# Spreading LayerNorm means and reciprocal roots over the partitions: one fp32 product each, or two float32r products

## The chip, the cores and the metric

One core of a Trainium2 chip runs the whole program in one launch. The metric is the device time of one execution in microseconds (us). The kernel before was run three times: 1618.89, 1621.05 and 1621.62 us, median 1621.05. One more execution was profiled; the trace in this document comes from it.

## What is computed

Two layers of a transformer block act on 256 latent and 256 context tokens with 1024 features, all in fp32. Each layer has a half feed-forward (FFN), a mixer (attention in layer 0, an mLSTM in layer 1) and a second half FFN. After each of these stands a LayerNorm:

```
def post_norm(h, delta, g, b):
    return layer_norm(DEEPNORM_ALPHA * h + delta, g, b)

def layer_norm(x, g, b):
    mu = mean(x); var = mean((x - mu)**2)
    return (x - mu) * rsqrt(var + LN_EPS) * g + b
```

The next stage multiplies the normalised rows, shifted and scaled by a modulation, with its weights. This document is about the means `mu` and the roots `rsqrt(var + eps)`.

## The kernel before, in words

**Layout.** The residual stream lies transposed in SBUF: tile `h` holds 8 blocks (`d`) of 128 features on the partitions by 512 tokens, of which columns 0 to 255 are the latent tokens (LAT) and 256 to 511 the context tokens (CTX). A norm therefore has to sum over partitions, and TensorE (PE) does this by a product with a 128x128 tile whose entries are all equal.

**Products.** A weight or an activation is split into a rounded part and a remainder, both of type float32r (`split`, L228 on ScalarE and L233 on VectorE), and `mm3` makes one accurate product of three float32r products (L244). A plain fp32 product appears in the trace as two MATMUL records and two weight loads. The products of the norms go through the lambda on L458, which also pins them to the order of the program on PE.

**Norms.** `norm` (from L453) is a generator; the other code advances it step by step. There are nine norms, one LAT and one CTX after each of the first four stages and a last one for LAT alone (`alone`). The letters in the step tables are its advances:

- `b` starts a LAT norm, `B` a CTX norm; the next letter `m` makes the product for the mean: `s1` holds the sum of the blocks (for LAT of the first seven, so that the norm can begin before the last block is there), and a 128x128 tile of 1/(1024-128) or 1/1024 sums it over the partitions and spreads the result to all 128 (L473).
- `c`, eight times, takes the mean from one block on VectorE (DVE, L478), squares it on ScalarE (ACT, L485) and adds up squares on DVE or GpSimd (POOL, L495).
- `v` makes the variance with products of one column (L503 to L507); a LAT norm also makes `dl`, the correction for the block left out (L510). Then the reciprocal root is worked out in eight small DVE instructions (L264 to L271), the roots are put on a diagonal `dg` (L521), and for LAT `dl` is copied out of PSUM (L527).
- `r` multiplies a tile of ones with `dg` (L535), which spreads the roots to all partitions.
- `x`, eight times, subtracts `dl` where DVE does it (L546) and makes the operands of the next stage: L551 on DVE, L552 on ACT, L553 on DVE.

**Order.** A planner orders the instructions of each engine by the order in the source and by when their inputs should be ready; pinned instructions keep the order of the source. Where the norm's steps fall among the products is written out by hand in tables. `TAILSTEP` (after the FFN stages) and `MTAILSTEP` (after attention) have keys (0 for LAT or 1 for CTX, block of outputs, index of the product triple); `LEADSTEP`, `ATTSTEP` and `MLSTEP` place the CTX norm among the first products of the next stage, with keys (unit, k). In this way a norm runs on DVE and ACT while PE goes on with the products of the stage that ends or begins.

**Addresses.** `SH`, `SHM` and `SHR` shift the weights in their tiles. Some FFN units go through `fast_in`, seven half products with operands that `fast_operands` lays into three tiles called `made`; behind these a tile of `FLIP` = 56 columns stands unused.

Of the kernel before, what the change touches and what calls it, by code (L numbers as in the profile page):

```python
# [18 lines left out]
P = 128  # L19
D = 1024  # L20
# [10 lines left out]
LINE = 16  # L31
# [57 lines left out]

FAST = {0: (99, 99), 1: (9, 5), 2: (9, 5)}  # L90
RESET = (14, 17, 20)
FLIP = 56
PIECES = 4
DOTS = {
    0: {**{("in", j): 3 for j in range(4, 21)}, **{("out", 0, d): 2 for d in range(8)}, **{("out", 1, d): 1 for d in range(4)}},
# [1 line left out]
    2: {**{("in", j): 3 if j < 3 else 2 for j in range(4)}, **{("out", 0, d): 3 for d in range(6)}, **{("out", 1, d): 2 for d in range(4)}},  # L97
}

TAILSTEP = {(0, 3, 1): 'bmccccccc', (1, 0, 2): 'c', (1, 0, 6): 'v', (1, 1, 9): 'rxxxxxxxx'}  # L100
MTAILSTEP = {(0, 7, 0): 'bmccccccc', (1, 0, 3): 'c', (1, 1, 0): 'v', (1, 6, 0): 'r', (1, 7, 0): 'xxxxxxxx'}

LASTROW = 9
LASTK = 6
# [1 line left out]


LEADSTEP = {
    1: {(0, 0): 'mcccccccc', (2, 1): 'v', (2, 5): 'rxxxxxxxx'},
    2: {(0, 5): 'mcccccccc', (2, 0): 'v', (2, 5): 'rxxxxxxxx'},  # L110
}
ATTSTEP = {(1, 1): 'mcccccccc', (3, 6): 'v', (5, 0): 'rxxxxxxxx'}
MLSTEP = {(1, 0): 'mcccccccc', (3, 4): 'v', (3, 7): 'rxxxxxxxx'}
MIXAT = 20
MLLEAD = 7
FILL = (-1, -1, 1, 7)
# [58 lines left out]
class Body:  # L175
# [99 lines left out]
    def setup(self):  # L275
        nc, a = self.nc, self.a
        self.cols = col = self.t([P, 3 * BLOCK // 2])
        for i, x in enumerate((1.0, 1.0 / D, 1.0 / (D - P), 0.5 / D)):
            nc.vector.memset(col[:, i : i + 1], x)
        self.mean1, self.half = col[:, 1:2], col[:, 3:4]  # L280
        self.ones, self.mean, self.most = (col[:, i : i + 1].broadcast_to([P, P]) for i in range(3))

        self.h = self.t([P, ND, T])
        self.xh = self.t([P, ND, T + BLOCK], F32R)
        self.xl = self.t([P, ND, T + BLOCK], F32R)
        self.ident = self.t([P, P])
        self.vec = self.t([P, V_N])
        self.mod = {}
        self.s1 = {}
        self.waiting = []  # L290
# [146 lines left out]
    def pin(self, ins):  # L437

        return self.tc.keep_in_program_order(ins)
# [14 lines left out]
    def norm(self, g, coef, keep=True, nxt=True, alone=False):  # L454


        nc, V, S = self.nc, self.nc.vector, self.nc.scalar
        mm = lambda *k, **kw: self.pin(nc.tensor.matmul(*k, **kw))  # L458
        t0, t1 = g
        w = t1 - t0  # L460
        n = w // P
        raw = alone and nxt
        v = 0 if t0 == 0 else 1
        most = g == LAT
        cols = lambda x, i: x[:, i * P : (i + 1) * P]
        if raw:
            ce = self.t([P, 2, ND], tag="modv", bufs=12)
            for i in range(2):
                V.tensor_copy(ce[:, i, :], coef()[1 + i][:, v, :])
            ce = ce.rearrange("p i d -> p d i")  # L470
            self.split(ce, self.xh[:, :, T : T + 2], self.xl[:, :, T : T + 2])
        m = self.ps()
        mm(m[:, :w], self.most if most else self.mean, self.s1[g], start=True, stop=True)  # L473
        sums = {}
        for d in range(ND):
            yield
# [2 lines left out]
            if raw:  # L479
                c = coef()[1][:, v, d : d + 1]  # L480
# [18 lines left out]
        last = self.h[:, ND - 1, t0:t1]  # L499
# [6 lines left out]
        x = self.small(n)  # L506
        pin = self.pin  # L507
        if most:
            dl = self.ps()
            mm(dl[:, :w], self.mean, last, start=True, stop=True)  # L510
            c2 = self.small(n)
            for i in range(n):
                c = var[:, n + i : n + i + 1]
                V.tensor_scalar(c2[:, i : i + 1], c, c, -0.5, ALU.mult, ALU.mult)
# [5 lines left out]
        dg = self.tmp(w)  # L520
        pin(V.tensor_tensor(  # L521
            out=dg.rearrange("p (n f) -> p n f", n=n), in0=self.ident[:, None, :].broadcast_to([P, n, P]),
            in1=r[:, :, None].broadcast_to([P, n, P]), op=ALU.mult,
        ))
        if most:
            dls = self.t([P, TL], tag="dl", bufs=1)
            pin(V.tensor_copy(dls, dl[:, :w]))  # L527
# [14 lines left out]
        for d in range(ND):  # L542
# [4 lines left out]
            ab, c, e = coef()  # L547
            x = self.tmp(w)
# [158 lines left out]
    def ffn(self, layer, s, gate, groups, side, start=None):  # L707
# [4 lines left out]
        with self.tc.tile_pool(name=f"ffn{li}", bufs=1) as gp:  # L712
# [35 lines left out]
            for hf in range(2):  # L748
# [1067 lines left out]
```

## Time and profile before

| | |
|---|---|
| median of three runs | 1621.05 us (1618.89 to 1621.62) |
| the profiled execution | 1623.23 us |
| its span, first to last instruction | 1621.5 us |
| PE busy | 1604.2 us, 99% |
| DVE busy | 1377.2 us, 85% |
| ACT busy | 759.1 us, 47% |
| POOL busy | 62.3 us, 4% |
| granted TensorE clock | 0.999 |

In the rows of the profile a line number is that of the kernel above. PE is TensorE multiplying, PEld its weight load, DVE VectorE, ACT ScalarE, POOL GpSimd. A group's row gives what it does, its shapes, how often, its busy time, the mean of one, and the idle time in front of it with what ended it. A busy PE is not PE at its peak, since matmuls overlap: how fast they follow each other is read from starts and counts.

### The profile page before, as it was taken

To read this page: it belongs to the slowest core of one execution; us is meant where nothing else is said; L and a number is where in the kernel's file an instruction comes from. 1 tells how busy PE (TensorE), PEld (TensorE's weight loads), DVE (VectorE), ACT (ScalarE), POOL (GpSimd) and SP (SyncE) were. 2 spreads that over 40 slices of the span, in tenths; PEclk is the share of its full clock that TensorE was granted. 3 is DMA by queue.
4 is the path that set the end of the run, shared out by engine and by line. 5 is a ranking of instruction groups with operands and counts; after the bars stand their busy time and mean duration, and the time that the engine had idled before them with its cause. 6 is when DMAs were issued, how large, how long until landed. Compare 5 with 4: busy or idle time off the path is not lost. (4 is left out here: it accounts for less than half of the span.)

```text
span 1621.5 us, 26945 instructions
## 1 busy us (share of the span) xinstructions
PE 1604.2 (99%) x10424; PEld 1453.2 (90%) x10424; DVE 1377.2 (85%) x2783; ACT 759.1 (47%) x1344; POOL 62.3 (4%) x77
## 2 busy tenths in 40 slices
PE   9999999999999999999999999999999999999998
PEld 7888888889988998989999998889989889999986
DVE  7789989878879879689986979689978958897687
ACT  6522132224676344515662435326643657566542
POOL 0000000001011200000000100000001000020000
PEclk9999999999999999999999999999999999999999
DMA  9667777642203342542254262743362332537552
GB/s 359 219 211 226 255 232 244 207 143 86 66 1 94 115 143 66 195 156 105 105 190 148 79 189 72 251 178 106 130 233 86 117 105 92 158 99 252 178 174 91
DMA packets 71648, 249.49 MB, mean 154 GB/s; under 512 B 7896, under 2 KB 10712, under 8 KB 71520
## 3 DMA queue, kind: packets, MB, share of 16 engines
q1 hardware_dynamic: 70944, 246.99, 46.6%
q8 instruction: 81, 1.33, 0.3%
q10 hardware_dynamic: 576, 0.79, 0.1%
q14 instruction: 47, 0.39, 0.1%
HBM read 246.69 MB, written 1.05 MB: 153 GB/s over the span
## 5 line engine op out<-in xcount | busy, mean ns | idle before, releaser
L244 PE MATMUL t<-t,t 128*128 128x256 f32 (+2 forms) x8484 | 1303.8, 315 | 4.9 <-ACT t L552 1.3
L244 PEld LDWEIGHTS t<-t,t 128*128 128x128 f32 x8484 | 1178.1, 188 | 116.4 <-DVE t L553 2.1
L228 ACT CAST t<-t 128x512 fp32r<-128x512 f32 (+3 forms) x573 | 436.4, 785 | 480.2 <-PE t L244 153.1
L233 DVE TENSOR_TENSOR t<-t,t 128x256 fp32r<-128x256 f32 (+3 forms) x792 | 516.7, 690 | 107.9 <-ACT t L228 106.0
L361 DVE SCALAR_TENSOR_TENSOR t<-t,t 128x1024 bf16<-128x1024 f32 x224 | 260.6, 1220 | 0.2
L974 PE MATMUL t<-t,t 128*128 128x256 f32 (+1 forms) x256 | 79.4, 310 | 0.1
L976 PE MATMUL t<-t,t 128*128 128x256 f32 (+1 forms) x256 | 78.6, 307 | 0.1
L975 PE MATMUL t<-t,t 128*128 128x256 f32 (+1 forms) x256 | 78.2, 306 | 0.0
L599 ACT ACTIVATE t<-t 128x256 f32<-128x256 f32 (+1 forms) x67 | 32.1, 484 | 92.8 <-PE t L244 91.9
L741 DVE SCALAR_TENSOR_TENSOR t<-t,t,t 128x256 f32<-128x256 f32 x96 | 42.7, 478 | 35.8 <-PE t L244 35.6
L495 POOL TENSOR_TENSOR t<-t,t 128x256 f32<-128x256 f32 x30 | 23.0, 768 | 1107.3 <-ACT t L485 1106.0
L902 PE MATMUL t<-t,t 128*128 128x512 f32 (+1 forms) x300 | 60.8, 364 | 0.4 <-DVE t L896 0.4
L902 PEld LDWEIGHTS t<-t,t 128*128 128x128 f32 x300 | 51.4, 189 | 9.7 <-DVE t L896 0.8
L1503 PE MATMUL t<-t,t 128*128 128x512 f32 (+2 forms) x276 | 55.8, 357 | 0.0
L1503 PEld LDWEIGHTS t<-t,t 128*128 128x128 f32 (+1 forms) x276 | 44.9, 183 | 11.1 <-issue 1.2
L653 DVE TENSOR_TENSOR t<-t,t 128x512 f32<-128x512 f32 x78 | 53.6, 687 | 0.7
L485 ACT ACTIVATE t<-t 128x256 f32<-128x256 f32 x72 | 26.3, 411 | 56.1 <-DVE t L478 56.1
L974 PEld LDWEIGHTS t<-t,t 128*128 128x128 f32 x256 | 48.3, 189 | 3.0 <-ACT t L552 0.3
L976 PEld LDWEIGHTS t<-t,t 128*128 128x128 f32 x256 | 48.1, 188 | 2.9 <-DVE t L553 0.3
L975 PEld LDWEIGHTS t<-t,t 128*128 128x128 f32 x256 | 48.1, 188 | 2.5
L600 DVE TENSOR_TENSOR t<-t,t 128x256 f32<-128x256 f32 (+1 forms) x67 | 36.3, 545 | 16.4 <-ACT t L599 10.9
L552 ACT ACTIVATE t<-t,t 128x256 fp32r<-128x256 f32 x72 | 32.8, 502 | 30.2 <-DVE t L551 30.2
(209 smaller groups left out, 1118.4 us busy)
## 6 DMA issues: line engine op xcount, KB each, us to landing
t<-in_ffn_in SPq DMA_DIRECT2D x168, 512.0 KB, 4.2
t<-in_ada_w SPq DMA_DIRECT2D x138, 512.0 KB, 4.4
t<-in_ffn_out SPq DMA_DIRECT2D x66, 512.0 KB, 4.4
t<-in_ffn_last SPq DMA_DIRECT2D x22, 512.0 KB, 3.6
t<-in_att_in SPq DMA_DIRECT2D x12, 512.0 KB, 3.6
t<-in_att_out SPq DMA_DIRECT2D x8, 512.0 KB, 3.5
t<-in_ml_qk SPq DMA_DIRECT2D x8, 512.0 KB, 4.0
t<-in_ml_v SPq DMA_DIRECT2D x8, 512.0 KB, 4.0
```

Source lines behind the costliest of these rows:

```text
L228: self.behind(self.nc.scalar.copy(h, x))
L233: self.behind(self.nc.vector.tensor_tensor(out=ls, in0=xs, in1=hs.bitcast(F32), op=ALU.subtract))
L244: mm = lambda *k, **kw: self.nc.tensor.matmul(*k, skip_group_check=not group, **kw)
L361: ins = nc.vector.scalar_tensor_tensor(self.tmp().bitcast(BF16), r, 1.0, self.cb[:, v, :], ALU.mult, ALU.mult, accum_out=to)
L600: V.tensor_tensor(out=sl, in0=sl, in1=pu[:, :n], op=ALU.mult)
L653: add = lambda o, x, y: V.tensor_tensor(out=o, in0=x, in1=y, op=ALU.add)
L741: V.scalar_tensor_tensor(z, y[:, gg[0] - t0 : gg[1] - t0], gate()[:, v, d : d + 1], z, ALU.mult, ALU.add)
L902: pin(nc.tensor.matmul(o, gs[g], ws[k][w][:, i : i + n], start=k == k0 and g == w == 0, stop=k == k1 - 1 and g == 1,))
L974: mm(o, self.xh[:, k, c], wh, start=k == 0, stop=False)
L975: mm(o, self.xh[:, k, c], wl, start=False, stop=False)
L976: mm(o, self.xl[:, k, c], wh, start=False, stop=k == ND - 1)
L1503: mm = lambda *k, **kw: pin(nc.tensor.matmul(*k, **kw))
```

## The change

Outside the `alone` norm, each fp32 product of a norm with 256 columns (the mean, `dl`, and the spread of the roots) becomes two float32r products that add up in PSUM, with a new float32r tile of ones as weights. For the means the sum is scaled and split before: ACT writes the rounded part, DVE the remainder. For the roots, the roots are split (a small copy and a small subtraction), and there are two diagonals. The steps of the tables are moved by some products, and the unused tile behind `made` is taken away. The new tile of ones is allocated ahead of `h`.

```
-FLIP = 56
-TAILSTEP = {(0, 3, 1): 'bmccccccc', (1, 0, 2): 'c', (1, 0, 6): 'v', (1, 1, 9): 'rxxxxxxxx'}
-MTAILSTEP = {(0, 7, 0): 'bmccccccc', (1, 0, 3): 'c', (1, 1, 0): 'v', (1, 6, 0): 'r', (1, 7, 0): 'xxxxxxxx'}
+TAILSTEP = {(0, 3, 4): 'bmccccccc', (1, 0, 4): 'c', (1, 0, 9): 'v', (1, 2, 3): 'rxxxxxxxx'}
+MTAILSTEP = {(0, 7, 3): 'bmccccccc', (1, 0, 3): 'c', (1, 1, 2): 'v', (1, 6, 0): 'r', (1, 7, 0): 'xxxxxxxx'}
...
-    1: {(0, 0): 'mcccccccc', (2, 1): 'v', (2, 5): 'rxxxxxxxx'},
-    2: {(0, 5): 'mcccccccc', (2, 0): 'v', (2, 5): 'rxxxxxxxx'},
+    1: {(0, 1): 'mcccccccc', (2, 0): 'v', (2, 5): 'rxxxxxxxx'},
+    2: {(0, 6): 'mcccccccc', (2, 0): 'v', (2, 6): 'rxxxxxxxx'},
...
-ATTSTEP = {(1, 1): 'mcccccccc', (3, 6): 'v', (5, 0): 'rxxxxxxxx'}
-MLSTEP = {(1, 0): 'mcccccccc', (3, 4): 'v', (3, 7): 'rxxxxxxxx'}
+ATTSTEP = {(1, 3): 'mcccccccc', (3, 6): 'v', (5, 2): 'rxxxxxxxx'}
+MLSTEP = {(1, 3): 'mcccccccc', (3, 4): 'v', (4, 0): 'rxxxxxxxx'}
...
+    def rounded(self, w):
+        x = self.t([P, 512], F32R, tag="tmp", bufs=6)
+        return x[:, :w], x[:, w : 2 * w]
...
+        self.one = self.t([P, LINE], F32R)[:, 0:1].broadcast_to([P, P])
+        nc.vector.tensor_copy(self.one[:, 0:1], col[:, 0:1])
...
+        def summed(o, x):
+            for i in range(2):
+                mm(o[:, :w], self.one, x[i], start=i == 0, stop=i == 1)
+
+        def halved(x, c):
+            h, l = self.rounded(w)
+            S.activation(h, x, AF.Copy, scale=c)
+            V.scalar_tensor_tensor(l, x, c, h.bitcast(F32), ALU.mult, ALU.subtract)
+            return h, l
...
-        mm(m[:, :w], self.most if most else self.mean, self.s1[g], start=True, stop=True)
+            summed(m, halved(self.s1[g], 1.0 / (D - P) if most else 1.0 / D))
...
-            mm(dl[:, :w], self.mean, last, start=True, stop=True)
+                summed(dl, halved(last, 1.0 / D))
...
+            dg = self.rounded(w)
+            rs = self.t([P, 16], F32R, tag="small", bufs=18)[:, :n].bitcast(F32), self.small(n)
+            pin(V.tensor_copy(rs[0].bitcast(F32R), r))
+            pin(V.tensor_tensor(out=rs[1], in0=r, in1=rs[0], op=ALU.subtract))
+        for o, x in zip(dg, rs):
+            pin(V.tensor_tensor(
...
-        mm(rb[:, :w], self.ones, dg, start=True, stop=True)
+            summed(rb, dg)
...
-        self.t([P, FLIP], pool=st)
```

More of the change, by code (lines that the diff above doesn't have):

```diff
@@ L471, in norm @@
             self.split(ce, self.xh[:, :, T : T + 2], self.xl[:, :, T : T + 2])
+        def summed(o, x):
[6 more added lines that the diff above has]
+            return h, l
         m = self.ps()
-        mm(m[:, :w], self.most if most else self.mean, self.s1[g], start=True, stop=True)
+        if alone:
+            mm(m[:, :w], self.most, self.s1[g], start=True, stop=True)
+        else:
+            summed(m, halved(self.s1[g], 1.0 / (D - P) if most else 1.0 / D))
         sums = {}
@@ L509, in norm @@
             dl = self.ps()
-            mm(dl[:, :w], self.mean, last, start=True, stop=True)
+            if alone:
+                mm(dl[:, :w], self.mean, last, start=True, stop=True)
+            else:
+                summed(dl, halved(last, 1.0 / D))
             c2 = self.small(n)
@@ L519, in norm @@
         r = self.rsqrt_half(x, n, pin)
[L520 to L524, printed above, removed]
+        if alone:
+            dg, rs = (self.tmp(w),), (r,)
+        else:
+            dg = self.rounded(w)
[4 more added lines that the diff above has]
+            pin(V.tensor_tensor(
+                out=o.rearrange("p (n f) -> p n f", n=n), in0=self.ident[:, None, :].broadcast_to([P, n, P]),
+                in1=x[:, :, None].broadcast_to([P, n, P]), op=ALU.mult,
+            ))
         if most:
@@ L534, in norm @@
         rb = self.ps()
-        mm(rb[:, :w], self.ones, dg, start=True, stop=True)
+        if alone:
+            mm(rb[:, :w], self.ones, dg[0], start=True, stop=True)
+        else:
+            summed(rb, dg)
         rs = self.t([P, TL], tag="rs", bufs=2) if keep and nxt else None
```

## The prediction

> **What bounds the kernel now.** I read the page first, then the groups by form, then PE's instructions in order of time around the norms, then what PE waited for and how busy DVE was there.
>
> ```profile
> span 1621.5 us, 26945 instructions
> PE 1604.2 (99%) x10424; PEld 1453.2 (90%) x10424; DVE 1377.2 (85%) x2783; ACT 759.1 (47%) x1344; POOL 62.3 (4%) x77
> ```
>
> PE is never idle for long, so time is won by giving it less to do, unless an engine that feeds it becomes late. DVE, at 85% over all, is the one that could.
>
> ```profile
> L458 PEld LDWEIGHTS t<-t,t 128*128 128x128 f32 x138 | 17.8, 190 | 4.2 <-DVE t L495 1.5 <-DVE t L435 0.8 <-DVE t L521 0.7
> L458 PE MATMUL t<-t,t 128*128 128x256 f32 x46 | 15.1, 411 | 1.1 <-DVE t L521 0.5 <-DVE t L1240 0.3
> L482 ACT ACTIVATE t<-t,t 128x256 fp32r<-128x256 f32 x8 | 4.0, 501 | 1.9 <-DVE t L478 1.9
> L483 DVE SCALAR_TENSOR_TENSOR t<-t,t,t 128x256 fp32r<-128x256 f32 x8 | 4.6, 579 | 0.0
> L521 DVE TENSOR_TENSOR t<-t,t 128x256 f32<-128x256 f32 x9 | 3.8, 422 | 0.4
> L270 DVE SCALAR_TENSOR_TENSOR t<-t,t 128x2 f32<-128x2 f32 x13 | 2.0, 155 | 0.1
> L435 DVE TENSOR_TENSOR t<-t,t 128x256 f32<-128x256 f32 x49 | 20.1, 421 | 0.5
> L546 DVE TENSOR_TENSOR t<-t,t 128x256 f32<-128x256 f32 x16 | 9.3, 606 | 0.1
> ```
>
> The first two rows are what the change is about: 46 records of 256 columns are 23 fp32 products of two records each: three in each of five LAT norms, two in each of four CTX norms. Their idle time is waiting for DVE. The change leaves the last LAT norm alone, so 20 products are replaced. The other rows are the nearest relatives of what is added.
>
> ```profile
> 559.44 2.44 PE L244 MATMUL t<-t,t 128*128 128x256 f32 x20
> 561.72 0.59 PE L458 MATMUL t<-t,t 128*128 128x256 f32 x2
> 561.96 1.05 PE L244 MATMUL t<-t,t 128*128 128x256 f32 x6
> 537.45 0.70 PE L458 MATMUL t<-t,t 128*128 128x256 f32 x2
> 537.80 4.95 PE L244 MATMUL t<-t,t 128*128 128x256 f32 x39
> 1105.84 10.36 PE L244 MATMUL t<-t,t 128*128 128x256 f32 x90
> 1446.93 33.24 PE L244 MATMUL t<-t,t 128*128 128x256 f32 x280 [0.26 <-DVE t L553]
> ```
>
> Columns are start, busy time and count. One record lasts about 0.28 us, but they overlap: 90 of them in 10.36 us start every (10.36 - 0.28) / 89 = 0.113 us. The last row shows a second pace of the same instruction, (33.24 - 0.28) / 279 = 0.118 us.
>
> **What an fp32 product costs.** Before the product that starts at 561.72, twenty rounded ones start every (2.44 - 0.28) / 19 = 0.114 us, so the next would have started at 559.44 + 20 x 0.114 = 561.72 too: this one had no wait. The next rounded group starts at 561.96, 0.24 later, and needs 1.05 us for six, where the pace of 0.118 gives 5 x 0.118 + 0.28 = 0.87: its second start is late by 0.18. The product costs 0.24 + 0.18 = 0.42 us of PE. Two rounded products cost 2 x 0.113 = 0.23, so 0.20 is saved, and **20 x 0.20 = 4.0 us** in all. No row shows a rounded product with a broadcast tile of ones. The ends are 0, if it brought its own unhidden weight load (190 ns, first row of L458), and 0.30, if a pair also frees the start that the fp32 weight load holds up; I take 0.20, since all other rounded products of this width keep the pace above.
>
> TensorE: Matmul & The Clock Gate, a page of the Trainium skill, gives in its section Back-to-back issue gap N / 2.4 + 2.5 ns for a warm array, an estimate of 0.109 us for 256 columns, which would leave the saving at 0.20 a product. It makes this gap depend on the columns and the clock alone; the trace disagrees, with paces of 0.113 and 0.118 at the same width and clock.
>
> **The pace after it.** Behind the fp32 product at 537.45, 39 products take 4.95 us; without the held-up first start of about 0.30 that is (4.95 - 0.28 - 0.30) / 37 = 0.118 us each. So the fp32 mean leaves PE in the slow pace until something sets it back. A rounded mean may keep 0.113 until the variance products, which stay fp32: 39 x 0.005 = 0.2 us in each of eight norms, 0 to 1.6; I take half, **0.8 us**.
>
> **The mean, later.** Now PE needs the last addition of L435; then it also needs ACT's rounded part and DVE's remainder. By L482 and L483 this is 0.50 + 0.58, so 1.1 us.
>
> ```profile
> 360.29 0.42 DVE L435 TENSOR_TENSOR t<-t,t 128x256 f32<-128x256 f32 x1
> 360.77 0.70 PE L458 MATMUL t<-t,t 128*128 128x256 f32 x2
> PEld t L458 <- DVE t L495: 0.8, 1, 0.8
> PEld t L976 <- DVE t L553: 0.3, 1, 0.3
> PEld t L458 <- DVE t L435: 0.3, 1, 0.3
> PEld t L974 <- ACT t L552: 0.3, 1, 0.3
> PEld t L458 <- DVE t L521: 0.7, 1, 0.7
> PEld t L244 <- ACT t L552: 1.0, 1, 1.0
> PEld t L458 <- DVE t L495: 0.6, 1, 0.6
> PEld t L458 <- DVE t L435: 0.5, 1, 0.5
> ```
>
> (The first two are the first norm's mean in order of time, the others PE's waits: four lines from 355 to 408 us, one from 882 to 932, three from 1233 to 1290.) The addition ends at 360.71, the product starts at 360.77: no slack. Each LAT mean moves by three triples, 9 x 0.113 = 1.02 us, so 0.1 is uncovered, 0.4 over four. The CTX means move by 6 products (0.68) in attention and the two FFNs and by 9 in the mLSTM. Attention's already waits 0.3 and 0.4 more is uncovered; the mLSTM's, which waits 0.5, gets 0.1 more; the FFNs' means are in no list of waits, and I take 0 for them, at most 0.4 each. Together 0.9. An ACT cast in front could add up to about 1 us to one mean.
>
> **`dl`.** Its split needs the last block, ready before the variance products; while these run DVE is idle:
>
> ```profile
> 368.69 0.35 DVE L514 TENSOR_SCALAR t<-t 128x1 f32<-128x1 f32 x2 [0.90 <-PE t L458]
> 372.81 0.42 DVE L521 TENSOR_TENSOR t<-t,t 128x256 f32<-128x256 f32 x1
> ```
>
> These 0.90 us hide the 0.58 on DVE, so I cost it at nothing; without the cover it is 0.58 in each of four norms, 2.3.
>
> **The roots.** From 368.69 to 372.81 + 0.42 the chain from variance to diagonal takes 4.5 us. It grows by two small instructions (2 x 0.16, L270) and a second diagonal (0.42, L521): 0.74. The distance from `v` to `r` grows by two triples (0.68) in three LAT norms, by 0.68 in three CTX norms and by 3 products in the mLSTM's, 0.34; after attention it shrinks by 0.68, and the missing 1.4 must come from the weight splits that lie between the small instructions. Uncovered: 0.06 in six norms, 0.4 in one, and between 0 and 1.4 after attention, where I take 0 because the planner can put those splits behind. I count **0.3** in all, and with the means **1.2 us** of new waits. The `x` steps move with `r`, by 5 triples or 1.7 us after the FFNs' LAT norms. What hides this is the rest of the CTX products: PE's waits for L552 and L553 above are those of CTX operands, and I cost it at nothing; without that cover it is up to 1.7 at the start of attention and of the mLSTM, 3.4.
>
> **DVE's load.** Per LAT norm 2 x 0.58 + 0.74 = 1.9 us, per CTX norm 1.3, in all 12.8 us; ACT gets 12 x 0.50 = 6.0.
>
> ```profile
> 370.00:394.00 24.00, 23.24 (x196) 22.56 (x194) 23.31 (x65) 13.49 (x26) 5.66 (x7) 1.00 0.31 98
> 550.00:568.00 18.00, 17.25 (x142) 16.74 (x140) 17.84 (x45) 9.42 (x20) 6.25 (x7) 1.00 0.18 60
> 900.00:917.00 17.00, 17.00 (x149) 16.95 (x148) 16.42 (x43) 8.63 (x18) 2.84 (x4) 1.00 0.20 63
> 1248.00:1267.00 19.00, 18.70 (x159) 18.33 (x157) 18.97 (x50) 12.11 (x27) 5.93 (x8) 1.00 0.23 71
> ```
>
> (Stretch, length, then busy PE, PEld, DVE, ACT, POOL.) Between the LAT roots and the CTX variance DVE is busy 76.5 of 78 us in the four transitions. The second LAT diagonal (0.42) and the CTX mean's remainder (0.58) fall there. What covers these 1.0 us is that part of DVE's work there splits weights PE uses later; if that cover is gone it costs 1.0 in each transition, 4.0.
>
> **Sum.** -4.0 - 0.8 + 1.2 = -3.6 us. The profiled execution took 1623.2 us, so the same execution would take 1619.6; the runs' median, 2.2 us below it, gives 1621.05 - 3.6 = **1617.5 us**. A measurement of this kernel can tell about 0.2%, 3.2 us, from no change. With the means' covers all holding and the full gain of pace it is 1615; with 2 us more of waits 1619.5.
>
> **Rivals.** *DVE takes it back.* The four full stretches above speak for it, the idle times outside them (0.90 before L514) against. If nothing can be put off, 4.0 us go to PE as waits on L495 at the CTX variance, where 0.8 and 0.6 are lost already: 1617.5 + 4.0 = 1621.5, no change; with the later `x` steps felt too, up to 1625. SBUF — State Buffer in the Trainium skill, section SBUF: two separate sides, speaks against the change here: a DVE instruction with two SBUF inputs and a GpSimd operation that reads SBUF hold one port in turn, each for its whole length. The trace agrees for L546, 606 ns beside POOL's work against 421 for L435; 20 of the new instructions are of this kind.
>
> *The fast products fall into the slow pace.* The new tile of ones moves everything behind it by 64 bytes, and `made` loses its 224 bytes of padding, so `made` and the weights no longer stand to each other as before. Each unit of `fast_in` has 7 x 12 = 84 products, 26 units run this way.
>
> ```profile
> L692 ACT COPY t<-t 128x256 f32<-128x256 f32 x26 | 9.7, 372 | 7.1 <-PE t L244 6.7
> ```
>
> Today they keep 0.113 (the row at 1105.84 is one). The row at 1446.93 shows that a pace, once slow, stays so for 33 us. If the new addresses decide for the slow one, 26 x 84 x 0.005 = 10.9 us come on top: 1617.5 + 10.9 = 1628.4, slower; if only the 36 products with `made` are slow, 4.7 and 1622.2. Against it: I see no row with these addresses, and no rule in the rows by which they should be slow.
>
> *The rounded pair is no cheaper,* the case that the change doesn't do what it says: saving 0, waits 1.2, 1622.3. Every rounded product of the trace speaks against it.
>
> **Chances.** Forecast 0.60, of which 0.45 lies beyond 0.2% and 0.15 within; DVE takes it back 0.20 (0.15 within, 0.05 slower); slow pace 0.17 (all counted as slower; of the milder form some would be within); no cheaper 0.03 (within). So faster 0.45, same 0.33, slower 0.22. The range runs from 1612.5 (the forecast with savings of 0.30 per product, 2 us more, and all gains of pace) to 1624.5, which holds most of the second case and the mild third, and leaves out the full slow pace. The likeliest case alone spans 1614 to 1620.
>
> **What would show it.** In the profile after, L458 should have 6 records of 256 columns left (the last norm's three products), and 40 new ones that follow their neighbours at 0.113 us. Waits of PE for the means should come from the new remainder instruction and be about 0.1 us for LAT, below 0.8 for CTX. The means' successors should keep 0.113 up to the variance. If PE's waits on L495 grow beyond 1 us each, the DVE rival holds; if 90 products of `fast_in` take 10.8 us, the pace rival. I am wrong if the span falls by under 2 us with neither of these seen.

## The result and the profile after

| | before | after |
|---|---|---|
| median of 6 runs | 1621.00 us (1618.89 to 1621.62) | 1629.43 us (1627.94 to 1632.12) |
| ratio of after to before | | 1.0056, 95% interval 1.0043 to 1.0069 |
| the profiled execution, its span | 1623.23, 1621.5 us | 1627.94, 1626.0 us |

The change made the kernel slower by 8.4 us by the medians and by 9.1 by the ratio; the forecast was 3.6 us faster, and the range ended at 1624.5. The two profiled executions are only 4.5 us apart in span: the one of before is slower than all six of its runs, the one of after the fastest of six.

The head of the page of after, and five rows of its groups by form:

```profile
span 1626.0 us, 26993 instructions
PE 1605.1 (99%) x10424; PEld 1453.4 (89%) x10424; DVE 1385.0 (85%) x2820; ACT 764.5 (47%) x1356; POOL 61.4 (4%) x77
```

```profile
L463 PEld LDWEIGHTS t<-t,t 128*128 128x128 f32 x138 | 18.6, 190 | 6.3 <-ACT t L483 3.1 <-DVE t L513 2.1 <-DVE t L484 0.6
L463 PE MATMUL t<-t,t 128*128 128x256 f32 x46 | 13.3, 328 | 2.3 <-ACT t L483 2.0
L483 ACT ACTIVATE t<-t 128x256 fp32r<-128x256 f32 x12 | 4.9, 411 | 40.8 <-DVE t L440 40.8
L484 DVE SCALAR_TENSOR_TENSOR t<-t,t 128x256 fp32r<-128x256 f32 x12 | 5.0, 417 | 3.1 <-ACT t L483 3.1
L549 DVE TENSOR_TENSOR t<-t,t 128x256 fp32r<-128x256 f32 x16 | 6.0, 418 | 0.0
```

L463 was L458, L247 was L244, L236 was L233, L231 was L228, L513 was L495, and the `x` steps are L582 to L584. The lines are those of after, unless a kernel is named. The 46 records of 256 columns are as many as before (6 fp32 ones and 40 rounded), so PE's count hides the change. The new instructions are cheaper than forecast, 417 ns for a remainder (L484) instead of 0.58 us, and DVE grew by 7.8 us, not 12.8. PE's waits at the norms changed more. From 355 to 408, 882 to 932 and 1233 to 1290 us (the stretches that the prediction quotes; four lines, two, and the first three):

```profile
PEld t L463 <- ACT t L483: 1.3, 2, 1.1
PEld t L463 <- DVE t L513: 1.0, 1, 1.0
PEld t L1004 <- ACT t L583: 0.7, 1, 0.7
PEld t L1006 <- DVE t L584: 0.5, 2, 0.3
PEld t L463 <- ACT t L483: 1.3, 1, 1.3
PEld t L463 <- DVE t L484: 0.5, 2, 0.3
PEld t L247 <- ACT t L583: 0.9, 2, 0.6
PEld t L247 <- DVE t L584: 0.7, 1, 0.7
PEld t L463 <- DVE t L513: 0.7, 1, 0.7
```

The waits that were put down to DVE's sums and diagonals (L435, L521 before) are gone. In their place stand waits put down to ACT's new rounded part: one LAT mean of 1.1 us, where 0.1 was forecast, and one CTX mean of 1.3, where 0 was. In the second case ACT's queue is not what is late. The cast at that time:

```profile
915.23 0.42 ACT L483 ACTIVATE t<-t 128x256 fp32r<-128x256 f32 x1 [1.74 <-DVE t L440]
```

ACT had waited 1.74 us for DVE's last addition (L440), and PE's product starts 0.47 us after the cast does. The transition from attention to the FFN, 523 to 603 us, is missing from the prediction's list. Before and after:

```profile
PEld t L244 <- ACT t L552: 0.7, 1, 0.7
PEld t L244 <- DVE t L233: 0.5, 1, 0.5
PEld t L244 <- ACT t L228: 0.3, 1, 0.3
```

```profile
PEld t L247 <- DVE t L236: 1.6, 2, 1.0
PEld t L247 <- DVE t L584: 1.3, 3, 0.8
PEld t L247 <- ACT t L583: 0.6, 1, 0.6
PEld t L463 <- DVE t L513: 0.5, 1, 0.5
```

L236 splits weights: here DVE is late even for weights, which the norm does not touch.

**By stretches.** All kernels here have 10424 PE records, and all but those of the moved steps stand in the same order, so the start of the same record can be compared in two traces. The table shows by how many us each kernel fell behind the first profile of before (minus: gained) in the stretch between two such records; the kernels other than before and after are explained further down.

| stretch of before, us | 345-440 | 523-603 | 603-880 | 880-953 | 953-1230 | 1230-1340 | rest | all |
|---|---|---|---|---|---|---|---|---|
| what it is | norms to attention | norms to layer 0's second FFN | `fast_in` | norms to layer 1's first FFN | `fast_in` | norms to the mLSTM | | |
| before again | 0.4 | 0.0 | -0.5 | 0.1 | -0.4 | 0.0 | -1.0 | -1.4 |
| after | 0.2 | 2.3 | 2.7 | -0.8 | 2.7 | -0.7 | -1.8 | 4.5 |
| after again | 0.0 | 4.0 | 2.7 | -0.8 | 2.1 | -0.3 | -1.7 | 6.1 |
| addresses alone | 0.1 | -0.2 | 2.7 | -0.4 | 3.1 | 0.0 | 0.9 | 6.3 |
| after, 40 columns | 3.0 | 4.1 | 0.8 | -0.9 | 0.0 | -0.3 | -1.1 | 5.7 |
| the same, old steps | 1.6 | 2.3 | -0.1 | -0.5 | -0.3 | 0.1 | -0.1 | 3.0 |
| rounded in norms 4 to 7 | -0.2 | -0.1 | -0.3 | -0.3 | -0.6 | -0.1 | -2.0 | -3.7 |
| side work alone | 0.1 | 1.6 | -0.5 | 1.7 | -0.1 | -0.8 | -1.2 | 0.9 |
| pairs alone | -0.2 | 0.0 | -0.5 | 1.6 | 0.0 | -1.0 | -1.9 | -2.1 |
| pairs, squares on DVE | -1.4 | 1.3 | 0.9 | -0.5 | -0.1 | 1.9 | -2.6 | -0.6 |
| squares on DVE | -1.2 | 1.0 | 0.9 | 0.1 | 0.1 | 0.0 | -0.3 | 0.6 |
| the mix | -0.5 | 0.1 | -0.5 | -0.9 | 0.7 | -1.5 | -0.1 | -2.7 |

The second profiles show what chance does: two executions of before differ by 0.5 at most in a stretch of the table (1.0 in the rest), two of after by 1.7 in one. That is a thin measure of chance: from 345 to 440 us *after, 40 columns* lost 3.0 us where two executions of after lost 0.2 and 0.0. One profile of a kernel is weaker evidence than its median, and the first profile of before was some 2 us slower than its median. The two stretches of `fast_in`, where the change put no instruction, hold 5.4 us of after's loss.

### The profile page after: what moved, and what is told of

The parts are those of the page before. It is cut to its first block, busy times and chain, and to the rows that moved or that the text cites. A ratio compares the mean times of both kernels' runs of the same rounds, so it can differ in the third digit from the quotient of the medians.

```text
span 1626.0 us, 26993 instructions
## 1 busy us (share of the span) xinstructions
PE 1605.1 (99%) x10424; PEld 1453.4 (89%) x10424; DVE 1385.0 (85%) x2820; ACT 764.5 (47%) x1356; POOL 61.4 (4%) x77
## 4 chain that ended last, share of the span: by engine, by line
PE 80%; DVE 14%; ACT 3%; issue 1%; DMA 1%; POOL 0%; DVEq 0%; SPq 0%; ACTq 0%; POOLq 0%
PE t L247 64%; PE t L1533 4%; PE t L932 4%; DVE t L236 4%; PE t L1005 2%; PE t L1004 2%; PE t L1006 2%; DVE t L584 1%; DVE t L582 1%; DVE t L366 1%; ACT t L231 1%; PE t L463 1%; DVE t L496 1%; ACT t L1104 0%; DVE t L440 0%
## 5 line engine op out<-in xcount | busy, mean ns | idle before, releaser
L247 PE MATMUL t<-t,t 128*128 128x256 f32 (+2 forms) x8484 | 1304.8, 314 | 6.2 <-DVE t L584 2.1
L247 PEld LDWEIGHTS t<-t,t 128*128 128x128 f32 x8484 | 1180.4, 188 | 117.6 <-DVE t L584 3.6
L231 ACT CAST t<-t 128x512 fp32r<-128x512 f32 (+3 forms) x573 | 435.4, 786 | 456.6 <-PE t L247 153.2
L236 DVE TENSOR_TENSOR t<-t,t 128x256 fp32r<-128x256 f32 (+3 forms) x792 | 517.9, 689 | 107.1 <-ACT t L231 104.9
L513 POOL TENSOR_TENSOR t<-t,t 128x256 f32<-128x256 f32 x30 | 23.1, 769 | 1118.6 <-ACT t L503 1117.4
L925 ACT ACTIVATE t<-t,t 128x1024 fp32r<-128x1024 f32 x22 | 25.1, 1152 | 27.0 <-DVE t L923 25.0
```

The source lines that it names most:

```text
L231: self.behind(self.nc.scalar.copy(h, x))
L236: self.behind(self.nc.vector.tensor_tensor(out=ls, in0=xs, in1=hs.bitcast(F32), op=ALU.subtract))
L247: mm = lambda *k, **kw: self.nc.tensor.matmul(*k, skip_group_check=not group, **kw)
```

## The experiments

Medians stand beside those of before on the same chip.

### The addresses

In the compiled programs `made` lies at 0 modulo 256 bytes in the kernel before and the weights that it meets at 64; after the change at 224 and 128. No trace shows addresses; the diff shows the shifts, 224 and 64 bytes (56 unused columns fewer behind `made`, one tile of 16 columns more ahead of `h`). Three kernels separate the address from the products. *Addresses alone* is before with after's addresses:

```
+        self.t([P, LINE], F32R)
         self.h = self.t([P, ND, T])
...
-        self.t([P, FLIP], pool=st)
```

> The kernel before with its fp32 products and its steps, but with the addresses of the kernel after: 16 unused columns ahead of h, and none behind made. Theory 1: 5 to 6 us slower than before, all of it in the two stretches of fast_in, 1626 to 1627. Theory 2: as before, 1621.

*After, 40 columns* and *24 columns* are the kernel after with unused columns again (`made` at 64, or at 128, with the weights at 128):

```
         x = self.t([P, 6 * n], F32R, pool=st)
+        self.t([P, 40], pool=st)
```

> The kernel after with 40 unused columns behind the three made tiles instead of none, so that they stand to the weights as they did before (64 bytes below them, modulo 256). Nothing else differs. Theory 1 (addresses): the 36 products with made in each of 26 units of fast_in go back from 0.119 to 0.113 us; 26 x 36 x 0.006 = 5.6 us less than after, so about 1624, still some 3 us over before, and the stretch 657 to 845 us gets back the 2.2 us that it lost. Theory 2 (waits): the address is beside the point and the loss is DVE's extra work in the transitions; the time stays at 1629.

> As e1_pad40, but with 24 unused columns: made then starts at a multiple of 64 bytes, as in the kernel before, but at the weights' own place modulo 256 and not 64 bytes below it. If what slows the products is that made is not at a multiple of 64 bytes, they run at 0.113 us and the time is that of e1_pad40; if it is where made stands to the weights, they stay slow, and the time is that of the kernel after, 1629, or near it.

And the 40 columns with the step tables of before:

> The kernel after with 40 unused columns behind made and with the step tables of the kernel before: the rounded products without the moves. Theory 1 says nothing on it beyond the 5.6 us. If the moves cover the longer chains, as the prediction took it, this is slower than e1_pad40 by the uncovered 1.1 us at eight means and 0.7 us at eight roots, less what was idle: 3 to 8 us. If the moves cost more than they cover (the later x operands and variances), it is faster than e1_pad40 by 1 to 3 us.

Measured, beside 1621.90 for before: addresses alone 1628.53 (ratio 1.0039, 1.0026 to 1.0051); 40 columns 1627.15 (1.0029, 1.0017 to 1.0041); 24 columns 1630.91 (1.0057, 1.0044 to 1.0070); 40 columns with the old steps 1625.99 (1.0030, 1.0018 to 1.0041). One unit of `fast_in` with its neighbours, 86 products (start, busy time, count), in before, after, addresses alone, 24 columns and 40 columns:

```profile
1110.48 9.95 PE L244 MATMUL t<-t,t 128*128 128x256 f32 x86
```

```profile
1115.46 10.20 PE L247 MATMUL t<-t,t 128*128 128x256 f32 x86
```

```profile
1113.39 10.20 PE L244 MATMUL t<-t,t 128*128 128x256 f32 x86
```

```profile
1117.73 10.19 PE L247 MATMUL t<-t,t 128*128 128x256 f32 x86
```

```profile
1117.10 9.95 PE L247 MATMUL t<-t,t 128*128 128x256 f32 x86
```

The same 86 products take 0.25 us longer in three kernels, 26 x 0.25 = 6.5 at most over all units; the table gives 5.4 for after and 5.8 for addresses alone. Most of it is in the 36 products with `made`: their starts are 113.4 ns apart on average (waits left out) in before and with 40 columns, 119 in the three others; the unit's other products go from 113.6 to 114.5. So it is shown that the addresses alone cost time without any new product, 5 to 6 us by the stretches, 4.2 to 8.3 by the interval of the runs. With `made` 64 bytes below its weights the pace is fast; level with them, or 96 above, it is slow. That 24 columns, too, put `made` on a multiple of 64 bytes and did not help excludes alignment to 64 alone. More placements were not tried, so no rule is shown.

What is left is the second finding: at good addresses the kernel is still slower than before by 0.3%, with either set of tables. The moved steps neither saved the 3 to 8 us that covering the longer chains was to be worth nor cost the 1 to 3: the two kernels are 1.2 us apart, within their intervals.

### Which products lose

A set of norms is chosen for each kind of product (norms counted from 0 in the order in which they begin, LAT even, CTX odd); the others stay fp32. Tables of before, 40 columns:

```
+MEANS, DLS, ROOTS = (0, 1, 2, 3, 4, 5, 6, 7), (0, 1, 2, 3, 4, 5, 6, 7), ()
...
-        if alone:
-            mm(m[:, :w], self.most, self.s1[g], start=True, stop=True)
+        if at not in MEANS:
+            mm(m[:, :w], self.most if most else self.mean, self.s1[g], start=True, stop=True)
```

> Only the means and dl are rounded (12 of the 20 products); the roots stay plain fp32; steps as before, 40 unused columns behind made, so that the fast products keep 0.113 us. The kernel with all 20 rounded at these steps and addresses took 1626.0 against 1621.9 before, 4.1 more, where a saving of 4.0 and a gain of pace of 0.8 were forecast: some 8.9 us of new waits have to be found. Theory A (the chain in front of the mean, ACT's rounded part in ACT's queue and DVE's remainder, is what is late): this part carries nearly all the waits, saves only 2.4 + 0.8, and is 4 to 5 us slower than before, 1626 to 1627. Theory B (the added DVE time is paid wherever it falls): means and dl are 7.0 of the 12.8 us added to DVE, so 4.8 of the waits, less 3.2 saved: 1.6 slower, 1623.5.

With only ROOTS filled:

> Only the spread of the roots is rounded (8 of the 20 products); means and dl are plain fp32 as before; steps as before, 40 unused columns behind made. Theory A: saves 8 x 0.20 = 1.6 and waits 0.3 more, 1620.5, 1.3 below before. Theory B: 5.9 of the 12.8 us on DVE, so 4.1 us of the waits, less 1.6 saved: 2.5 slower, 1624.4.

With MEANS and ROOTS filled, but not DLS:

> As the kernel with all rounded at the steps of before and 40 unused columns, but dl as a plain fp32 product in its four norms. If dl's split is hidden in DVE's idle time, only its saving of 4 x 0.20 is lost: 0.8 above that kernel, 4.9 above before, 1626.2. Theory B: 4 x 0.58 of the 12.8 us on DVE go as well, 1.6 us of waits, so 0.8 below that kernel, 3.3 above before, 1624.6.

Measured: means and `dl` 1623.91 beside 1621.26 (1.0015, 1.0006 to 1.0024); roots 1623.79 (1.0013, 1.0004 to 1.0022); all but `dl` 1625.82 beside 1621.24 (1.0022, 1.0013 to 1.0031). Each part loses by itself, roots as much as means. Counted from before on the same chip, they lose 2.6 and 2.5 us: theory A, which has only the means late, missed by 1.4 to 2.4 and by 3.8 us, theory B by 1.0 and by nothing. For `dl` the two forecasts are 1.6 us apart and the interval is 2.9 wide: left open.

The step tables of after with everything else as before:

> The kernel before with the steps of the kernel after, all products plain fp32, addresses as before. The moves alone. Theory A: the later means and roots find their operands ready, so PE's short waits ahead of them (some 2 us over four norms) shrink and the later operands of the next stage take as much back: within 1.5 us of before, 1620.5 to 1623.5. Theory C (the later steps are what costs, since the operands of the next stage come up to 1.7 us later in each of four transitions): 3 us or more slower, 1625 or above.

1621.34 beside 1621.26 (1.0000, 0.9991 to 1.0008): with fp32 products the later steps cost nothing, as the prediction had it, and theory C falls.

### The pairs alone, and the side work alone

The change has two halves: PE is given less to do, and ACT and DVE more. They were run apart. *Side work alone* is the kernel before plus all new ACT and DVE instructions, whose results nobody reads:

```
+        if not alone:
+            halved(self.s1[g], 1.0 / (D - P) if most else 1.0 / D)
         mm(m[:, :w], self.most if most else self.mean, self.s1[g], start=True, stop=True)
```

> The kernel before with its plain fp32 products, steps and addresses, and beside them all that the change adds on ACT and DVE for 20 products (rounded part, remainder, split roots, second diagonal), written to tiles that no product reads: its outputs are those of before, the extra work is for nothing. Theory B (the added DVE time is paid as PE's waits for what DVE does later): all the waits and none of the savings, 8.9 us slower, 1630. Theory A (the products wait for a longer chain of operands): no product needs this work, so under 1 us, 1622.

*Pairs alone* leaves out the remainders. It has two rounded products for each mean and each spread of roots, both with one operand that the old DVE instruction writes rounded (the cut is against the kernel after):

```
-            summed(m, halved(self.s1[g], 1.0 / (D - P) if most else 1.0 / D))
+            summed(m, self.s1[g], self.most2 if most else self.mean2)
```

> The pairs without their split: means and root spreads are two float32r products each (16 of the 20; dl stays fp32), but both products of a pair read one operand that the same DVE instruction as before wrote, rounded, with a weight of half the size. It leaves out the remainders, so means and roots are only as exact as float32r; no work is added on ACT or DVE, and no chain is longer. Steps as before, fast products at their fast place. If a pair saves 0.20 us and brings back some of the pace: 16 x 0.20 + 0.6 = 3.8 below before, 1617.4; the longer chain then costs about 4.8 us in the full change. If PE's time between norms is set by what DVE delivers and a pair saves nothing that counts: no change, 1621.2, and the longer chain costs next to nothing.

Side work alone: 1625.75 beside 1621.24 (1.0025, 1.0016 to 1.0035). Pairs alone: 1620.19 beside 1621.19 (0.9995, 0.9986 to 1.0004). So about half of the 8.9 us of waits that theory B asked for come with work whose results no product reads, 2.6 to 5.7 us by the interval; theory A's less than 1 is excluded. (Two of the new small instructions still stand in DVE's pinned order ahead of the diagonal that the product reads, so a little of the longer chain is in this kernel.) By the profile the loss lies in two stretches, 523 to 603 us and 880 to 953; in the second PE waits 1.2 us for the diagonal and 1.1 for the last sum of squares. And the saving is not there: 1.0 us instead of 3.8, and at most 2.3 by the interval. The sum of the two ratios, 1.0020, lies within the interval of the whole at these addresses, 1.0018 to 1.0041 (old steps); so a further cost of the longer chain, up to 0.2%, is neither shown nor excluded by them.

Where the saving goes is seen around the CTX norm after layer 0's second FFN. PE in order of time, first before, then pairs alone (there L458 is L469, L495 is L520, L485 is L510 and L228 is L232):

```profile
909.35 0.59 PE L458 MATMUL t<-t,t 128*128 128x256 f32 x2
909.59 8.01 PE L244 MATMUL t<-t,t 128*128 128x256 f32 x66
917.58 1.05 PE L458 MATMUL t<-t,t 128*128 128x1 f32 x8
```

```profile
907.62 0.39 PE L469 MATMUL t<-t,t 128*128 128x256 f32 x2
907.84 7.75 PE L248 MATMUL t<-t,t 128*128 128x256 f32 x66
917.34 1.05 PE L469 MATMUL t<-t,t 128*128 128x1 f32 x8 [1.75 <-DVE t L520]
```

The pair does what the sum said: the next product starts 0.22 us after it (0.24 before) without a held-up second start, and the 66 that follow take 7.75 instead of 8.01. The mean is 1.73 us earlier than before. But the variance is only 0.24 earlier: the gain is spent in a wait of 1.75 for the last sum of squares. ACT at the same time, before and pairs alone:

```profile
913.78 1.06 ACT L228 CAST t<-t 128x1024 fp32r<-128x1024 f32 x1 [0.39 <-DMA t<-in_ffn_in]
914.74 1.33 ACT L485 ACTIVATE t<-t 128x256 f32<-128x256 f32 x4
```

```profile
913.57 1.05 ACT L232 CAST t<-t 128x1024 fp32r<-128x1024 f32 x1 [2.06 <-DMA t<-in_ffn_in]
914.52 1.33 ACT L510 ACTIVATE t<-t 128x256 f32<-128x256 f32 x4
```

The last four squares (L485, L510) stand in ACT's queue behind the cast of a block of weights, and this waits for a DMA: ACT idles 2.06 us instead of 0.39, and the cast begins only 0.21 us earlier. The same cast ahead of attention, in the second profile of before and in pairs alone, begins at the same time within 0.06 us, though the squares in front of it begin 0.65 us earlier:

```profile
390.50 1.05 ACT L228 CAST t<-t 128x1024 fp32r<-128x1024 f32 x1 [0.88 <-DMA t<-in_att_in]
```

```profile
390.44 1.05 ACT L232 CAST t<-t 128x1024 fp32r<-128x1024 f32 x1 [1.35 <-DMA t<-in_att_in]
```

So the last four squares of each CTX norm were moved to DVE, with the pairs and without them:

```
-            S.activation(q, z, AF.Square)
+            if g == CTX and d >= ND // 2:
+                V.tensor_tensor(out=q, in0=z, in1=z, op=ALU.mult)
+            else:
+                S.activation(q, z, AF.Square)
```

> The pairs without their split (remainders left out, as before), and the last four squares of each CTX norm made by DVE instead of ACT, so that they do not stand behind a cast that waits for a DMA; 16 x 0.42 = 6.7 us more on DVE, 2.3 of them in time in which DVE waited for ACT after layer 0's second FFN. Theory D (ACT's queue behind the DMA holds up the CTX variance): PE's waits for the last sum of squares fall from 4.4 to 2 us or less, and the time by 2 us, to 1618.2. Theory B (DVE's time decides): the added 6.7 us cost 2.1, as the 12.8 us of side work cost 4.1: 1622.3.

> The kernel before with the last four squares of each CTX norm made by DVE instead of ACT, plain fp32 products, nothing else. Theory D: before loses only 1.6 us ahead of these variances, of which up to 1 can be won, and DVE's added time takes some back: 1620.2 to 1621.7; the pairs win 2 us or more against this kernel where they won 1.0 against before. Theory B: 2.1 slower, 1623.3, and the pairs win 1.0 as before.

Pairs with squares on DVE: 1624.21 beside 1621.16 (1.0017, 1.0008 to 1.0026). Squares on DVE, fp32 products: 1622.39 (1.0007, 0.9998 to 1.0016). Theory D was right about the wait and wrong about the time: pairs with squares on DVE take 4.0 us more than pairs alone, and against squares on DVE with fp32 products, where theory D had the pairs win 2 us or more and theory B 1.0, they lose 1.8 (the intervals overlap). PE's waits at the last sum (L520, here L523) were, in pairs alone in the norms to attention, to layer 1's first FFN and to the mLSTM:

```profile
PEld t L469 <- DVE t L520: 1.3, 1, 1.3
PEld t L469 <- DVE t L520: 2.0, 1, 2.0
PEld t L469 <- DVE t L520: 1.1, 1, 1.1
```

In pairs with squares on DVE (to layer 1's first FFN, to the mLSTM, then the waits for weights after attention and before the mLSTM):

```profile
PEld t L469 <- DVE t L523: 0.5, 1, 0.5
PEld t L469 <- DVE t L523: 1.2, 1, 1.2
PEld t L248 <- DVE t L237: 2.3, 1, 2.3
PEld t L248 <- DVE t L237: 2.6, 1, 2.6
```

The waits at the variance fell from 4.4 to 1.7, and the stretches to attention and to layer 1's first FFN gained 1.2 and 2.1 us against pairs alone. In the two other transitions waits for split weights grew from 0.7 and 0.2 to 2.3 and 2.6 and took it back. The busy times there (stretch, length, PE, PEld, DVE, ACT, POOL) show DVE full:

```profile
550.00:568.00 18.00, 15.80 (x128) 15.00 (x127) 18.00 (x46) 9.30 (x19) 4.67 (x6) 1.00 0.12 32
1248.00:1267.00 19.00, 17.53 (x153) 17.14 (x151) 19.00 (x51) 10.61 (x22) 5.36 (x7) 1.00 0.20 66
```

DVE has not a tenth of a microsecond left; in before it was busy 17.84 and 18.97 us there. So the traces speak for two different things that hold PE to its old times: a DMA through ACT's queue at two transitions, DVE's full schedule at the two others. This reading rests on single profiles, and it is not the whole: moving the squares won 1.2 us ahead of attention with fp32 products as well, so the pairs themselves hardly won more there.

One rival was not tested. The granted clock listed with the runs averages 0.9988 in the four kernels whose norms keep fp32 products (addresses alone, moves, side work, squares on DVE; 36 runs), as in before, and 0.9981 in the eleven that round products in all eight norms (94 runs): 0.9982 in pairs alone, 0.9975 in pairs with squares on DVE. If the whole span follows the clock, an estimate from these figures, 0.0007 x 1621 = 1.1 us, would be a good part of the missing 2.8, and 0.0013 x 1621 = 2.1 as much as the pairs lose against squares on DVE. The clock is listed to three digits only; whether the rounded products lower it, and what that costs, is not shown.

### The chain in front of the product

Remainders and second diagonals on POOL, to relieve DVE (the cut shows the remainder):

```
-            V.scalar_tensor_tensor(l, x, c, h.bitcast(F32), ALU.mult, ALU.subtract)
+            y = self.tmp(w)
+            S.activation(y, x, AF.Copy, scale=c)
+            nc.gpsimd.tensor_tensor(out=l, in0=y, in1=h.bitcast(F32), op=ALU.subtract)
```

> The kernel with all rounded at the steps of before and 40 unused columns (1626.0 where before took 1621.9), but with the remainders and the second diagonals on POOL: ACT writes the scaled sum as well (12 x 0.50 us more on ACT), POOL subtracts (12 x 0.77) and makes 8 diagonals (8 x 0.87). 10.4 of the 12.8 us leave DVE. Theory B: 7.2 of the 8.9 us of waits go, 3.1 below before, 1618.2. Theory A: the chain in front of each mean grows by 0.7 us and that of each root by 0.45, 8 x 0.7 + 8 x 0.45 = 9.2 more waits than with DVE, 1634; half of it where there is slack, 1630.

1631.80 beside 1621.24 (1.0066, 1.0054 to 1.0079). PE's weight loads at norms in the kernel with the same steps and addresses (40 columns, old steps), then in this one:

```profile
L463 PEld LDWEIGHTS t<-t,t 128*128 128x128 f32 x138 | 19.3, 190 | 8.0 <-ACT t L483 3.5 <-DVE t L513 1.8 <-PE t L247 1.5
L463 PEld LDWEIGHTS t<-t,t 128*128 128x128 f32 x138 | 19.0, 190 | 15.6 <-POOL t L486 6.3 <-ACT t L483 3.1 <-DVE t L515 2.6
```

Idle time there went from 8.0 us to 15.6, and the largest part, 6.3, is behind POOL's remainder. Theory B failed here: with less work on DVE the kernel is 6 us slower than with it there, where the chain in front of each product is longer. So both count.

The rounded part of the means on DVE instead of ACT:

```
-            S.activation(h, x, AF.Copy, scale=c)
+            if x is last_sum:
+                V.tensor_scalar(h, x, c, None, ALU.mult)
+            else:
+                S.activation(h, x, AF.Copy, scale=c)
```

> All rounded, steps as before, 40 unused columns, but the rounded part of each mean is written by DVE instead of ACT (dl's still by ACT). If ACT's queue holds up the first mean (its wait of 1.45 us is put down to ACT, which is at a Silu on 1024 columns just then), that wait falls to the length of two DVE instructions, 0.8 to 0.9 us, for 8 x 0.4 = 3.2 us more on DVE: in time between 1 us less and 1 us more than the 4.1 above before. If it is the length of the chain and not the queue, the wait stays at 1.4.

1623.19 beside 1621.19 (1.0017, 1.0007 to 1.0026), against 1.0030 with the casts on ACT: the intervals overlap, the trace decides. The first mean in after, ACT, then PE:

```profile
361.15 1.06 ACT L322 ACTIVATE t<-t 128x1024 f32<-128x1024 f32 x1 [0.50 <-DMA t<-in_c]
362.11 0.40 ACT L483 ACTIVATE t<-t 128x256 fp32r<-128x256 f32 x1
```

```profile
362.56 0.38 PE L463 MATMUL t<-t,t 128*128 128x256 f32 x1 [0.90 <-ACT t L483]
```

With the cast on DVE, DVE and PE:

```profile
360.51 0.42 DVE L440 TENSOR_TENSOR t<-t,t 128x256 f32<-128x256 f32 x1
360.97 0.29 DVE L486 TENSOR_SCALAR t<-t 128x256 fp32r<-128x256 f32 x1
```

```profile
361.31 0.39 PE L463 MATMUL t<-t,t 128*128 128x256 f32 x1
```

On ACT the cast waits for a Silu, and the Silu for the DMA of the condition. On DVE it follows the last sum at once, and the first product 0.05 us later. So that wait is the queue's, not the cast's. It is one mean: at the CTX mean after layer 0's second FFN PE waits 1.2 us with the cast on DVE, as it did with the cast on ACT (1.1 at the same steps), since there DVE's last addition comes late.

### Mixes, and the spread of profiles

All rounded, but only in norms 4 to 7, at the steps of before; and a mix with fp32 around attention, and means and `dl` rounded in 4 to 7 and roots in 4 and 5 alone, at the steps of after for norms 0, 1, 4 and 5 and of before for the others:

```
+MEANS, DLS, ROOTS = (4, 5, 6, 7), (4, 6), (4, 5)
```

> All three kinds rounded, but only in the four norms after layer 0's second FFN and layer 1's first FFN; the norms around attention stay fp32; steps as before, 40 unused columns behind made. In the kernel with all norms rounded at these steps the stretches of these four norms took 0.5 and 1.0 us less than before and the start of the mLSTM 0.4 to 1.1 more, those around attention 1.6 and 2.3 more. If each stretch stands for itself (theory A): 1 us below before, 1620.9, and well below the kernel with all rounded. If the added work is only paid elsewhere (theory B): half of 4.1, 2 slower, 1624.

> A mix: the norms around attention (after layer 0's first FFN and after attention) with plain fp32 products, at the later steps after the FFN and at the steps of before after attention; all rounded and at the later steps after layer 0's second FFN; means and dl rounded, roots fp32, at the steps of before after layer 1's first FFN; 40 unused columns. From the stretches of the other kernels against before: about 0.5 less at the first, 0 at the second, 0.9 less at the third, 1.4 less at the last, no delay at the start of the mLSTM: 2.8 in all, 1618.5. If these differences of single profiled executions are chance, no change, 1621.3.

Norms 4 to 7: 1620.38 beside 1621.26 (0.9997, 0.9988 to 1.0006). That is theory A's forecast, and theory B's 2 us slower is excluded: with the products rounded in these four norms nothing is lost. At good addresses the loss of the whole change therefore lies in norms 0 to 3, around attention, which is where the table has it for *the same, old steps*: 1.6 and 2.3 us. The net loss is not spread evenly over the norms. The mix: 1619.97 beside 1621.24 (0.9990, 0.9981 to 0.9999), the only kernel with an interval below 1, by less than the 0.2% that was called measurable; of sixteen such intervals one may do so by chance. A mix with squares on DVE at two transitions alone was not tried.

Second profiles of before and after:

> The kernel before once more, for a second profile. If the gain of about 1 us that most of the other kernels show in the stretch from 1230 to 1300 us belongs to their changes, this one shows the 1623.2 us execution's time there again; if it belongs to that one execution, this one is faster there by about 1 us.

> The kernel after once more, for a second profile: the fast products start every 0.119 us again, and the mean of the first norm waits for ACT by 1 to 1.9 us, as the DMAs of the condition happen to land.

Before again gained nothing from 1230 to 1340 us, so the gain of most kernels there is theirs. After again has the slow `fast_in`, but waits for ACT at the first mean by only 0.8 us.

## Why the prediction was wrong

Three terms of the sum failed. The addresses were put at nothing and cost 5 to 6 us. The saving and the recovered pace, 4.0 and 0.8, were counted as time of the kernel, and pairs alone, where 3.8 was due, won 1.0. New waits were put at 1.2 us, and the new ACT and DVE work alone cost 4.1. The three measured ratios (1.0039, 0.9995 without `dl`, 1.0025) add up to 1.0059; the whole change has 1.0056.

**The pace of the fast products.** The rival was named, with a chance of 0.17, and its milder form (only the 36 products with `made`) priced at 4.7 us. This form came true, at 5 to 6. What failed is the argument against it, "I see no row with these addresses, and no rule in the rows by which they should be slow": the absence of a row was taken as evidence. That `made` and its weights would move against each other was plain from the diff; at what place the pace turns was not. The price was right because it went by the two paces that the trace showed.

**"20 x 0.20 = 4.0 us in all".** The size of a product was right: 0.22 for a pair. The pace, too, recovered. Behind the LAT mean after attention, in after:

```profile
539.13 3.68 PE L247 MATMUL t<-t,t 128*128 128x256 f32 x31
```

These start every (3.68 - 0.28) / 30 = 0.113 us, where before had 0.118. The failure is to count these as time of the kernel. Pairs alone won 1.0 of 3.8 us. The rival *DVE takes it back* had the place right, waits on L495 at the CTX variance, 4.4 us there in pairs alone against 1.6 in before (0.8, 0.6 and 0.2 in three of the four transitions). It had half of the mechanism: at two of four transitions the squares were late through ACT's queue and a DMA, and DVE waited for them; the prediction looked at ACT's queue for the means only. Why the rest of the saving is missing stays open, the granted clock included.

**"1.2 us of new waits".** Side work alone cost 4.1 us (2.6 to 5.7 by its interval), though DVE's real addition in after, 7.8 us, was smaller than the 12.8 of the sum. "Part of DVE's work there splits weights PE uses later" is one step that failed: after attention PE waits for just these splits (1.6 us on L236 in after), a transition whose waits were not in the list. "An ACT cast in front could add up to about 1 us to one mean" was taken at nothing: it was 1.1 us at the first mean (0.8 in after again). At the CTX mean after layer 0's second FFN the 1.3 is in part DVE's last addition, late behind its other work, and the stretch as a whole still gained 0.8 in after.

**What held, and what was not tried.** `x` steps moved at no cost. The remainder takes 417 ns in the mean, but that says nothing against the port that DVE and POOL share by the Trainium skill (SBUF — State Buffer, section SBUF: two separate sides): in the trace of after no remainder and no diagonal runs beside a POOL instruction. The additions of L440 do in five of 58 cases and take 956 ns there in the mean, 418 elsewhere, which agrees with the rule.

Two bounds were added up wrongly: 1617.5 less 2 us of savings and 0.8 of pace is 1614.7, not 1612.5, and with the means' covers and the full pace 1615.8, not 1615. Neither bears on the outcome.

The rivals were given chances as if one excluded the other. Addresses (5 to 6) and DVE's case (1621.5 to 1625) add up to 1626.5 to 1631, and 1629.4 lies in it.

## What to carry to other kernels

On an engine that is 99% busy, as PE is here, shorter work may win only up to the next operand: before counting it, follow each product's operand back through the queues of its makers to the first thing that PE does not set, such as a DMA landing, and ask how early that is. Test the saving and the price apart: the new products with no new work behind them, and the new work with nobody reading it. If a diff moves an allocation, treat the addresses as a change of its own and run them alone.

## What the runs showed of the hardware

Two float32r products of 256 columns that differ by nothing but the place of their moving operand start 113 or 119 ns apart, at a granted clock of 0.997 to 0.999 (9.95 and 10.19 us for the same 86 products, in kernels that differ by 64 bytes of padding). TensorE: Matmul & The Clock Gate in the Trainium skill, section Back-to-back issue gap, gives for an isolated gap, not for a stream as the prediction took it, a formula of columns and clock alone (an estimate of 109 ns), and says that in a stream weight loads and products set it together. Neither has the place of the operand in it, which these rows show to count.

In after, five DVE additions of two 128x256 tiles that met work of POOL took 0.96 us in the mean, the 53 others of that line 0.42.
